# Delta-rule heads of a hybrid layer in two overlapped streams, decays masked by a minimum

## The chip, the cores and the metric

One core of a Trainium2 chip runs the whole program in one launch. The metric is the device time of one execution in microseconds; the median of three runs of the kernel before is 2117.78 us (2115.77 to 2118.18). Engines: TensorE (PE), VectorE (DVE), ScalarE (ACT), GpSimd (POOL) and SyncE (SP), which only issues DMAs. Each works through its own list of instructions in order and waits on semaphores.

## What is computed

512 positions of width 1024 go through a hybrid layer and two more layers with feed-forward blocks. All is fp32. Only the mixer of the first layer, `mix1`, bears on the change. It projects its normalized input, convolves over time, and runs two recurrences: a gated delta rule (8 heads) and a state-space model (SSD, 16 heads in 2 groups).

```python
def gdn_chunked(q, k, v, g, beta):   # heads of 128 x 128
    ...
    gc = jnp.cumsum(g, axis=-1)
    decay = jnp.exp(jnp.where(causal, gc[..., :, None] - gc[..., None, :], -jnp.inf))
    kb = k * beta[..., None]
    a_in = jnp.einsum("bhnid,bhnjd->bhnij", kb, k) * decay
    lmat = jnp.where(strict, a_in, 0.0) + jnp.eye(CHUNK, dtype=a_in.dtype)
    ...
    sol = lax.linalg.triangular_solve(lmat, rhs, left_side=True, lower=True, unit_diagonal=True)
    ...
    def step(state, xs):
        v_new = u_i - jnp.einsum("bhcd,bhde->bhce", w_i, state)
        o = jnp.einsum("bhcd,bhde->bhce", q_i, state) + jnp.einsum("bhij,bhje->bhie", qk_i, v_new)
        state = state * gl[..., None, None] + jnp.einsum("bhcd,bhce->bhde", k_i, v_new)
...
o_a = rms_norm(o_a, gdn_norm_w) * jax.nn.silu(z_a)
...
y = (ssd_chunked(xs_, dt, a_neg, bm, cm) + ssd_d * xs_) * jax.nn.silu(z_s)   # then rms_norm by group
mix = jnp.concatenate([o_a, o_s], axis=-1) @ w_out
x = x + rms_norm(mix, post_mix_norm)
```

## The kernel before

Activations lie as 8 blocks of 128 features by 512 positions, or, by "token", as 128 positions by 4 chunks. A projection multiplies fp32 data that are split into a high and a low part: three 512-column matmuls for each of 8 blocks (`mm3`, L214 to L216), 24 in all. Its weights come by `wload`: SP loads 512 KB (wr, L196), ACT casts the high part (wh, L202), DVE subtracts for the low part (wl, L205). `split1` does the same for activations (L295, L296).

`head_proj(h)` makes q, k and v of a head: projection, scaling on DVE (u, L466), a convolution with its first tap on ACT (L474) and three on DVE (L479), and SiLU on ACT (L691). `z_proj` makes the gate of a head, `zs_evac` those of SSD, `xbc` the inputs of SSD.

`gdn(h0, qkv)` is a generator for a pair of heads, cut by `yield` into stages. *Set-up:* k and q are transposed and squared (`sumsq`, L712), `kd` is k scaled by its decay (L729); `decay` makes exp(min(gc row - gc column, 0)) (L683, L684); B is k times k by decay and beta (L750); its 16x16 diagonal blocks are summed out (L754, L756), written to DRAM and read back rearranged (bdd: L757, L762, one write and eight reads on SP). Then PT is q times k by decay (L770), masked to the upper triangle on POOL (L771), and `nkv` is v scaled (L780). *Substitution:* 15 steps of two small DVE instructions solve the 16x16 blocks (L791, L792), and DVE spreads the result into Y (L801); PE transposes it to X (pX, L798). *Doubling:* X and Y grow to blocks of 32, 64 and 128 by products on PE (pT, pU, pY) with steps on DVE and ACT between them (L814 to L837). *Recurrence:* over four chunks, per head, PE forms k times state, DVE subtracts (r, L853), PE applies Y, DVE scales (vt, L856), PE forms the new state, DVE adds (L862 for chunk 0, L864); po is the output. *Output:* squares on ACT (L872), a root on DVE, product (L877), transposition (pfo, L880), gate (L882).

The loop over pairs drives a generator to the end of its substitution's inputs, and then, one stage at a time, writes projections between its stages as the table GF says: the next pair's heads, the z gates and the SSD gates all beside the substitution, doubling and recurrence of the same pair:

```python
GF = [[0], [1], [2, 3], []]
...
            for n in range(3):
                next(g)
            for n, fill in enumerate(GF):
                for x in fill:
                    ...
                if next(g, 1):
                    break
```

Then come the SSD inputs of group 0 (`ssd_proj`), `ssd_prep` (CB masked by a triangle on DVE, L947; x times dt on DVE, L957; xd = that by a decay on POOL, L960), `ssd_core` (states pS, L971; masked decays; y products py, L999, and po, L1002; norm; transposition pf, L1022), the inputs of group 1, and the output projection in three parts: `w_o1a` (delta-rule heads, splits alternating between DVE and POOL by PA), group 1's core, `w_o1b` (group 0, splits by PB_), `w_o1c` (group 1).

The order of the text is not the order of the engines: a list scheduler takes the instructions as they are written, with priorities by place (raised inside `high_priority`), and fixes one list for each engine. Tiles come from pools with a fixed number of buffers, so a buffer that is late to come free delays its next user.

Of the kernel before, what the change touches and what calls it, by code (L numbers as in the profile page):

```python
# [1 line left out]

# [38 lines left out]
for _n, _c in PV:  # L41
# [49 lines left out]
class Prog:  # L91
    def __init__(s, ctx, tc, a):
# [512 lines left out]
    def mix1(s, after):  # L605
# [290 lines left out]
        sc.activation(zs[0][:, :, 0:256], zs[0][:, :, 0:256], AF.Silu)  # L896

        nxt = [head_proj(0), head_proj(1)]
        for h0 in range(0, GDN_H, 2):
            g, nxt = gdn(h0, nxt), []  # L900
            for n in range(3):
                next(g)
            more = h0 + 2 < GDN_H
            for n, fill in enumerate(GF):
                for x in fill:
                    if x >= 2:
                        z_proj(h0 + x - 2)
                    elif more:
                        nxt.append(head_proj(h0 + 2 + x))
                    else:  # L910
                        for m in range(1 + x, 2 + 2 * x):
                            s.proj_tm([a["w_zs"][m - 1, 0], a["w_zs"][m - 1, 1]], acts, zs_evac(m))
                if next(g, 1):
                    break
            for _ in g:
                pass
# [651 lines left out]
```

## Time and profile before

| | before |
|---|---|
| median of 3 runs | 2117.78 us (2115.77 to 2118.18) |
| the profiled execution | 2123.84 us |
| its span, first to last instruction | 2122.1 us |
| busy: PE / DVE / ACT / POOL | 2078.7 / 1380.9 / 943.2 / 80.4 us |
| mean granted TensorE clock | 0.989 of 2.4 GHz |
| chain that ended last, by engine | PE 82%, DVE 8%, ACT 4%, DMA 3% |

The profiled execution is one more run, 0.3% above the median; its times are what the rows below give. A busy PE counts the time in which a matmul is under way, also at the lower clock; a granted clock of 1.00 is 2.4 GHz, 0.5 is 1.2 GHz, and values between them are means over a window. "Idle before <- releaser" says how long an engine stood still ahead of an instruction, and what it waited for.

### The profile page before, as it was taken

The numbers are of one execution on the slowest core, as the hardware profiler recorded it, in microseconds if no ns is written. First come the engines' busy times: TensorE is split into PE (matmuls) and PEld (weight loads), VectorE is DVE, ScalarE is ACT, GpSimd is POOL, SyncE is SP. The second block draws the span as 40 slices with busy tenths as digits, with TensorE's granted clock in tenths as the row PEclk, the third lists the DMA queues.
The fourth block names the chain that finished last, engine by engine and source line by source line (L and its number), as shares of the span: only waits on it lengthen the run. The fifth ranks groups of instructions, "written<-read, shape, count | busy, mean of one in ns | idle before, by whom it ended". The sixth has DMA issues, their size and how long they took to land.

```text
span 2122.1 us, 27151 instructions
## 1 busy us (share of the span) xinstructions
PE 2078.7 (98%) x10558; PEld 1734.2 (82%) x10558; DVE 1380.9 (65%) x2383; ACT 943.2 (44%) x1555; POOL 80.4 (4%) x79
## 2 busy tenths in 40 slices
PE   8989999999999999999999999999999999999999
PEld 7877898878888888888776888888879888888887
DVE  7858767787598776237997777753333676777621
ACT  7535435456455444235665444432252444444321
POOL 0000000111000000100001000001100010000000
PEclk9989999999999999999999999999999999999999
DMA  5323122133223223332111233233222122332332
GB/s 176 97 65 106 36 81 91 61 109 129 70 87 102 92 98 93 94 96 95 50 50 60 80 109 99 93 91 99 91 78 90 60 80 72 117 99 92 97 114 65
DMA packets 60358, 189.16 MB, mean 89 GB/s; under 512 B 7901, under 2 KB 13277, under 8 KB 60230
## 3 DMA queue, kind: packets, MB, share of 16 engines
q1 hardware_dynamic: 57874, 180.75, 26.6%
q0 software_dynamic: 2032, 6.59, 1.0%
q8 instruction: 83, 1.36, 0.3%
q14 instruction: 45, 0.37, 0.1%
q10 hardware_dynamic: 324, 0.09, 0.0%
HBM read 184.99 MB, written 2.41 MB: 88 GB/s over the span
## 4 chain that ended last, share of the span: by engine, by line
PE 82%; DVE 8%; ACT 4%; DMA 3%; issue 1%; POOL 0%; SPq 0%; ACTq 0%; DVEq 0%; POOLq 0%
PE pp L214 24%; PE pp L215 24%; PE pp L216 24%; DVE wl L205 2%; DMA wr<-in_w_qkvz 1%; DVE qkv L479 1%; PE pz L1124 1%; PE pU L819 1%; PE pT L812 1%; PE pS L1367 1%; ACT wh L202 1%; PE po L1376 1%; DMA a<-bdd 1%; ACT s L712 1%; PE py L999 0%
## 5 line engine op out<-in xcount | busy, mean ns | idle before, releaser
L214 PE MATMUL pp<-a,wh 128*128 128x512 f32 (+1 forms) x2128 | 823.1, 388 | 8.5 <-ACT a L326 2.4
L215 PE MATMUL pp<-a,wh 128*128 128x512 f32 (+1 forms) x2128 | 818.6, 385 | 4.2 <-DVE a L296 2.6
L216 PE MATMUL pp<-a,wl 128*128 128x512 f32 (+1 forms) x2128 | 817.5, 385 | 1.7 <-DVE wl L205 1.7
L202 ACT CAST wh<-wr 128x1024 fp32r<-128x1024 f32 (+3 forms) x327 | 336.6, 1031 | 513.7 <-PE pp L215 385.6
L205 DVE TENSOR_TENSOR wl<-wr,wh 128x1024 fp32r<-128x1024 f32 (+3 forms) x327 | 393.2, 1203 | 222.4 <-ACT wh L202 218.7
L214 PEld LDWEIGHTS pp<-a,wh 128*128 128x128 f32 x2128 | 402.7, 190 | 93.2 <-issue 6.8
L215 PEld LDWEIGHTS pp<-a,wh 128*128 128x128 f32 x2128 | 403.5, 190 | 84.0 <-DVE a L296 4.0
L216 PEld LDWEIGHTS pp<-a,wl 128*128 128x128 f32 x2128 | 403.0, 189 | 80.1 <-DVE wl L205 3.3
L466 DVE TENSOR_TENSOR u<-pp,rb 128x512 f32<-128x512 f32 x198 | 135.9, 688 | 165.8 <-PE pp L216 165.3
L479 DVE SCALAR_TENSOR_TENSOR c<-u,pv,c 128x511 f32<-128x511 f32 (+1 forms) x264 | 196.5, 748 | 3.9
L216 PE MATMUL pp<-t,wl 128*128 128x512 f32 (+1 forms) x336 | 130.9, 389 | 0.0
L214 PE MATMUL pp<-t,wh 128*128 128x512 f32 (+1 forms) x336 | 130.8, 389 | 0.0
L215 PE MATMUL pp<-t,wh 128*128 128x512 f32 (+1 forms) x336 | 129.7, 386 | 0.0
L214 PE MATMUL pp<-wh,a 128*128 128x256 f32 (+2 forms) x384 | 112.7, 295 | 7.4 <-ACT wh L355 4.8
L215 PE MATMUL pp<-wl,a 128*128 128x256 f32 (+2 forms) x384 | 112.2, 293 | 0.0
L216 PE MATMUL pp<-wh,a 128*128 128x256 f32 (+2 forms) x384 | 111.9, 292 | 0.0
L476 ACT ACTIVATE c<-u,pv 128x512 f32<-128x512 f32 x132 | 107.5, 815 | 9.0 <-DVE u L466 8.5
L499 ACT ACTIVATE c<-c 128x512 f32<-128x512 f32 x66 | 41.7, 632 | 106.5 <-DVE c L479 106.4
L214 PEld LDWEIGHTS pp<-wh,a 128*128 128x128 f32 x384 | 74.1, 194 | 9.7 <-ACT wh L355 4.8
L295 ACT CAST t<-c 128x512 fp32r<-128x512 f32 x42 | 26.1, 621 | 114.9 <-DVE c L500 114.9
L216 PEld LDWEIGHTS pp<-wh,a 128*128 128x128 f32 x384 | 74.3, 194 | 1.5 <-issue 1.4
L215 PEld LDWEIGHTS pp<-wl,a 128*128 128x128 f32 x384 | 74.2, 193 | 1.6 <-issue 1.2
(343 smaller groups left out, 2180.3 us busy)
## 6 DMA issues: line engine op xcount, KB each, us to landing
wr<-in_w_up SPq DMA_DIRECT2D x132, 512.0 KB
wr<-in_w_dn SPq DMA_DIRECT2D x48, 448.0 KB
wr<-in_w_qkvz SPq DMA_DIRECT2D x32, 512.0 KB
wr<-in_w_dn SPq DMA_DIRECT2D x24, 512.0 KB
t<-gcd POOLq DMA_DIRECT2D x24, 256.0 KB, 4.2
wr<-in_w_xbc SPq DMA_DIRECT2D x12, 512.0 KB
a<-bdd SPq DMA_DIRECT2D x32, 128.0 KB
wr<-in_w_o1a SPq DMA_DIRECT2D x8, 512.0 KB
```

The source lines that it names most:

```text
L202: nc.scalar.copy(hi[:, :f], raw[:, :f])
L205: e.tensor_tensor(lo[:, :f], raw[:, :f], hi[:, :f], ALU.subtract)
L214: mm(out, l[0], r[0], start=first, stop=False)
L215: mm(out, l[0], r[1], start=False, stop=False)
L216: mm(out, l[1], r[0], start=False, stop=last)
L295: nc.scalar.copy(hi, src)
L466: s.nc.vector.tensor_tensor(u, ps, rb, ALU.mult)
L476: nc.scalar.activation(c, u, AF.Identity, scale=w(taps - 1), bias=bias)
L479: nc.vector.scalar_tensor_tensor(c[:, sh:], u[:, :S - sh], w(j), c[:, sh:], ALU.mult, ALU.add)
L499: nc.scalar.activation(g, g, AF.Silu)
L712: sc.activation(j, pk[:, c, :], AF.Square, accum_out=out[:, col + c:col + c + 1])
L812: te.matmul(pT[:, c * 64:(c + 1) * 64], B[i][:, ch(c)], left(X[i][:, ch(c)], b), start=True, stop=True)
```

## The change

Line numbers of the changed kernel are 5 higher at L210, 14 to 20 higher in `gdn` and 31 higher at the end of SSD.

1. *Two streams.* The main loop drives two generators: g does the doubling, recurrence and output of pair p, n the set-up and substitution of pair p + 1, a stage of each in turn. GF is now a table by pair and stage of what is projected where: "h" a head, "z" a gate of a delta-rule head, "s" SSD gates, "x" SSD inputs. Group 0's SSD inputs are thereby projected beside the last pair.
2. *Decay.* L683 was subtract and minimum with 0; now it is one instruction with a tile `upto` (0 on and below the causal bound, -1e30 above) for the minimum, so the mask lies in the decay. The POOL mask of PT (L771) goes, and the DVE product that made CB becomes a copy on ACT.
3. *ACT for DVE.* `kd` and `nkv` are made by four scaled copies of 128 columns on ACT instead of one DVE product of 512, in tiles of another pool.
4. *POOL to DVE.* xd and four of the splits for the output projection.
5. *Priorities.* Cast and split of weights (HL), scaling of SSD inputs (HX), the splits and the first row of `w_o1a` (HA) are raised; the first head's split comes before group 0's core, the splits for `w_o1b` right after it.
6. *Tiles.* z0, the first SSD gates, lie in two tiles of the "act" pool; the triangle for the cumulative sums has its own load.

Instructions on DVE 2385 to 2379, on ACT 1432 to 1505, on POOL 84 to 64, on SP 403 to 404.

```diff
-    "mix1": [("tri", 128), ("lev", 2 * 64), ("b16", 8), ("i16", 16)],
+    "tri": [("tri", 128)],
+    "mix1": [("upto", 128), ("lev", 2 * 64), ("b16", 8), ("i16", 16)],
...
+    c["upto"] = np.where(i[:, None] <= i[None, :], 0.0, -1e30)
...
-        nc.scalar.copy(hi[:, :f], raw[:, :f])
...
-        e.tensor_tensor(lo[:, :f], raw[:, :f], hi[:, :f], ALU.subtract)
+        with s.tc.high_priority(offset=s.ahead):
+            nc.scalar.copy(hi[:, :f], raw[:, :f])
+            nc.vector.tensor_tensor(lo[:, :f], raw[:, :f], hi[:, :f], ALU.subtract)
...
-                v.tensor_scalar(r[:, c * P:(c + 1) * P], r[:, c * P:(c + 1) * P], gc3[:, c, h:h + 1], 0.0, ALU.subtract, ALU.min)
+                v.scalar_tensor_tensor(r[:, cs], r[:, cs], gc3[:, c, h:h + 1], s.c("upto"), ALU.subtract, ALU.min)
...
-                v.tensor_tensor(v3(kd[i]), ptk, dec3[:, :, h].unsqueeze(2).to_broadcast([P, NT, P]), ALU.mult)
+                for c in range(NT):
+                    sc.activation(kd[i][:, ch(c)], ptk[:, c, :], AF.Copy, scale=dec3[:, c, h:h + 1])
...
-                nc.gpsimd.tensor_tensor(v3(PT[i]), v3(PT[i]), tri_b, ALU.mult)
...
-                v.tensor_tensor(v3(nkv[i]), to_tok(vf[i]), nk[:, 4 * i:4 * i + 4].unsqueeze(2).to_broadcast([P, NT, P]), ALU.mult)
+                ptv = to_tok(vf[i])
+                for c in range(NT):
+                    sc.activation(nkv[i][:, ch(c)], ptv[:, c, :], AF.Copy, scale=nk[:, 4 * i + c:4 * i + c + 1])
...
+        heads, fs0 = {}, []
+        fill(0, 0)
+        g = gdn(0, [heads.pop(h)[0] for h in range(2)])
+        for n in range(4):
+            next(g)
+            fill(0, n + 1)
+        for p in range(4):
+            h1 = 2 * p + 2
+            n = gdn(h1, [heads.pop(h)[0] for h in (h1, h1 + 1)]) if p < 3 else iter([1] * 9)
+            for i in range(4):
+                next(g)
+                next(n)
+                fill(p + 1, i)
+            for _ in g:
+                pass
+            fill(p + 1, 4)
+            g = n
...
-            v.tensor_tensor(v3(CB), v3(pc), tri_b, ALU.mult)
+            sc.copy(CB, pc)
...
-                nc.gpsimd.tensor_tensor(v4(x3, 3), v4(x1)[:, 0:3], hb(dec3[:, 0:3, csl], 3), ALU.mult)
+                v.tensor_tensor(v4(x3, 3), v4(x1)[:, 0:3], hb(dec3[:, 0:3, csl], 3), ALU.mult)
...
+        pa = [s.split1(f) for f in oa[:NE]]
+        ssd_core(0, *ssd_prep(0, fs0, [s.act(F32) for _ in range(4)]))
+        hb4 = s.x8(F32R)
...
-GF = [[0], [1], [2, 3], []]
-PA = 0
-PB_ = 2
-WP = 0
+GF = ((("h0", "h1"), (), ("h2",), (), ("h3",)),
+      (("h4",), ("z0",), ("h5",), ("z1",), ()),
+      (("h6",), ("z2",), ("h7",), ("z3",), ()),
+      (("z4",), ("s1",), ("z5",), ("x8",), ("x10", "x0")),
+      (("z6",), ("s2",), ("z7",), ("s3",), ("x1", "x2", "x3")))
...
+NE = 1
+HA = 300
+HX = 300
+HL = 100
```

*First place: ACT in the first pair's substitution, before and now.* wh is a weight cast, qkv<-u,pv a convolution's first tap, qkv<-qkv its SiLU; x_617 is nkv of the first pair. The casts wh_1102 (before) and wh_1186 (now) are those of the first load that SP issues behind the bdd round trip.

```order
L474 ACTIVATE qkv_888<-u_886,pv 128x512
L691 ACTIVATE qkv_849<-qkv_849 128x512
L202 CAST wh_1102<-wr_1100 128x1024
L691 ACTIVATE qkv_888<-qkv_888 128x512
L474 ACTIVATE qkv_978<-u_976,pv 128x512
L691 ACTIVATE qkv_978<-qkv_978 128x512
L202 CAST wh_1136<-wr_1134 128x1024
```

Now, on ACT at the same place:

```order
L479 ACTIVATE qkv_853<-u_851,pv 128x512
L705 ACTIVATE qkv_814<-qkv_814 128x512
L705 ACTIVATE qkv_853<-qkv_853 128x512
L479 ACTIVATE qkv_992<-u_990,pv 128x512
L800 ACTIVATE x_617<-ps_890,s_886 128x128 x4
L800 ACTIVATE x_617<-ps_899,s_886 128x128 x4
L209 CAST wh_1186<-wr_1184 128x1024
L705 ACTIVATE qkv_992<-qkv_992 128x512
```

The tap of qkv_978 stood two rows behind the cast; that of qkv_992 (q of the fourth head in both) stands three rows ahead of it.

*Second place: DVE in the first pair's recurrence.* s<-rc are the recurrence's steps (r, vt, state), L801 and L821 the last substitution rows.

```order
L837 TENSOR_SCALAR t_929<-pU_1220 64x4x64
L837 TENSOR_SCALAR t_930<-pU_1226 64x4x64
L856 TENSOR_SCALAR s_1237<-rc_1235,s_672 128x128
L856 TENSOR_SCALAR s_1245<-rc_1243,s_672 128x128
L862 COPY s_1240<-rc_1235 128x128
L862 COPY s_1248<-rc_1243 128x128
L853 SCALAR_TENSOR_TENSOR s_1253<-rc_1251,s_426,t_763 128x128
L853 SCALAR_TENSOR_TENSOR s_1265<-rc_1263,s_426,t_770 128x128
L856 TENSOR_SCALAR s_1256<-rc_1251,s_672 128x128
L856 TENSOR_SCALAR s_1268<-rc_1263,s_672 128x128
```

Now, on DVE, where chunk 1 begins:

```order
L821 TENSOR_TENSOR t_1674<-s_1639,cmix_283 128x512
L821 TENSOR_TENSOR t_1675<-s_1639,cmix_283 128x512
L806 COPY s_3083<-cmix_283 128x128
L873 SCALAR_TENSOR_TENSOR s_1726<-rc_1724,s_432,x_617 128x128
L873 SCALAR_TENSOR_TENSOR s_1738<-rc_1736,s_432,x_617 128x128
L876 TENSOR_SCALAR s_1729<-rc_1724,s_684 128x128
L876 TENSOR_SCALAR s_1741<-rc_1736,s_684 128x128
L471 TENSOR_TENSOR u_1977<-pp_1952,rb_366 128x512
L884 SCALAR_TENSOR_TENSOR s_1732<-s_1628,s_430,rc_1724 128x128
L884 SCALAR_TENSOR_TENSOR s_1744<-s_1636,s_430,rc_1736 128x128
L210 TENSOR_TENSOR wl_2268<-wr_2265,wh_2267 128x1024
L873 SCALAR_TENSOR_TENSOR s_1750<-rc_1748,s_432,x_617 128x128
```

Before, r of chunk 1 (L853) followed chunk 0 directly, with the next pair not yet set up. Now it (L873) stands behind the last substitution rows of the next pair (t_1674, t_1675); foreign rows among the ten are u_1977 and wl_2268.

*Third place: PE at the end of SSD group 1.* pf is the transposition of group 1's output, pp_4803 and pp_4856 products of `w_o1a`, pp_5162 (before), pp_5199 and pp_5247 (now) products of `w_o1b`.

```order
L214 MATMUL pp_4803<-a_4562,wh_4799 128x512
L1022 MATMUL pf_5111<-cst,a_4527 128x128 x2
L215 MATMUL pp_4803<-a_4563,wh_4799 128x512
L216 MATMUL pp_4803<-a_4562,wl_4800 128x512
L1022 MATMUL pf_5111<-cst,a_4527 128x128 x2
L1022 MATMUL pf_5122<-cst,a_4528 128x128 x4
L1022 MATMUL pf_5133<-cst,a_4529 128x128 x4
L214 MATMUL pp_5162<-a_5140,wh_5158 128x512
```

Now, on PE, behind the last po of group 1:

```order
L1033 MATMUL po_5116<-t_4953,xbc_4421 128x128
L221 MATMUL pp_4856<-a_4615,wl_4853 128x512
L1033 MATMUL po_5116<-t_4961,xbc_4421 128x128
L219 MATMUL pp_5199<-x_4336,wh_5195 128x512
L220 MATMUL pp_5199<-t_4337,wh_5195 128x512
```

And on PE where the first pf stands:

```order
L219 MATMUL pp_5247<-x_4336,wh_5229 128x512
L220 MATMUL pp_5247<-t_4340,wh_5229 128x512
L221 MATMUL pp_5247<-x_4336,wl_5230 128x512
L1053 MATMUL pf_5153<-cst,a_4583 128x128
L219 MATMUL pp_5247<-x_4336,wh_5229 128x512
L1053 MATMUL pf_5153<-cst,a_4583 128x128
```

Before, `w_o1b` began behind the last pf. Now 42 of its matmuls stand ahead of the first pf, and the others lie among the pf (the two pieces are the start and the end of those 42).

## Rows read from the trace of the kernel before

**Rows 1.** The page, part 1: busy us, share of the span, instructions.

```profile
PE 2078.7 (98%) x10558; PEld 1734.2 (82%) x10558; DVE 1380.9 (65%) x2383; ACT 943.2 (44%) x1555; POOL 80.4 (4%) x79
```

**Rows 2.** Window: length, busy PE PEld DVE ACT POOL, PEclk, DMA share, GB/s.

```profile
40.00:540.00 500.00, 476.91 (x2804) 407.61 (x2803) 372.77 (x861) 246.06 (x574) 39.67 (x48) 0.97 0.28 87
```

**Rows 3.** Windows by stage of the first layer, the same columns.

```profile
113.00:138.00 25.00, 24.21 (x146) 21.59 (x146) 7.04 (x15) 5.93 (x10) 0.54 (x1) 0.73 0.17 50
138.00:160.00 22.00, 21.87 (x133) 19.14 (x132) 17.47 (x47) 7.85 (x23) 0.00 (x0) 1.00 0.17 53
...
183.00:207.00 24.00, 21.46 (x95) 17.46 (x93) 20.96 (x51) 10.21 (x15) 0.00 (x0) 1.00 0.54 165
207.00:228.00 21.00, 20.46 (x148) 17.59 (x149) 8.77 (x16) 5.91 (x10) 0.54 (x1) 0.92 0.14 34
...
347.00:374.00 27.00, 24.61 (x102) 19.29 (x100) 21.76 (x51) 10.25 (x13) 0.00 (x0) 0.94 0.47 156
415.00:457.00 42.00, 40.93 (x250) 35.48 (x249) 37.77 (x82) 24.33 (x57) 10.86 (x17) 1.00 0.25 80
457.00:473.00 16.00, 11.34 (x35) 7.22 (x34) 16.00 (x30) 9.33 (x24) 5.45 (x3) 0.85 0.40 133
473.00:500.00 27.00, 25.97 (x145) 21.22 (x144) 16.24 (x33) 20.46 (x41) 6.88 (x9) 0.97 0.38 127
528.00:540.00 12.00, 9.66 (x33) 6.14 (x32) 4.00 (x6) 11.90 (x29) 0.00 (x0) 0.72 0.19 57
```

**Rows 4.** Timeline of PE, first and second X: start, us, instruction, [idle <- releaser].

```profile
107.83 0.39 PE L215 MATMUL pp<-a,wh 128*128 128x512 f32 x1
108.06 0.39 PE L216 MATMUL pp<-a,wl 128*128 128x512 f32 x1
113.79 1.11 PE L798 MATMUL pX<-cst,t 128*128 128x128 f32 x4 [5.35 <-DVE t L801]
...
207.54 0.65 PE L798 MATMUL pX<-cst,t 128*128 128x128 f32 x4 [3.08 <-DVE t L801]
```

**Rows 5.** Timeline of DVE in the first substitution.

```profile
94.64 0.75 DVE L479 SCALAR_TENSOR_TENSOR qkv<-u,pv,qkv 128x511 f32<-128x511 f32 x1 [4.03 <-ACT qkv L474]
95.31 0.25 DVE L791 TENSOR_TENSOR s<-a,s 128x96 f32<-128x96 f32 x1
```

**Rows 6.** Timeline of ACT in the first substitution.

```profile
92.42 1.05 ACT L202 CAST wh<-wr 128x1024 fp32r<-128x1024 f32 x1 [5.71 <-DMA wr<-in_w_qkvz]
```

**Rows 7.** Timeline of SP in the first substitution.

```profile
80.61 5.08 SPq L762 DMA_DIRECT2D a<-bdd  x8
85.81 5.03 SPq L196 DMA_DIRECT2D wr<-in_w_qkvz  x2
```

**Rows 8.** Waits of SP, 40 to 540 us: total us, times, longest.

```profile
SPq L757 <- DVE s L756: 65.5, 4, 24.2
```

**Rows 9.** By line: count, ns min/median/max, first and last start, forms.

```profile
L683 DVE TENSOR_SCALAR t<-t,s x96: 273/282/590, 67.7 to 511.9; 128x128 f32<-128x128 f32 x96
...
L853 DVE SCALAR_TENSOR_TENSOR s<-rc,s,t x24: 344/351/354, 140.6 to 402.9; 128x128 f32<-128x128 f32 x24
...
L479 DVE SCALAR_TENSOR_TENSOR xbc<-u,pv,xbc x36: 730/746/1756, 357.0 to 470.8; 128x511 f32<-128x511 f32 x12, 128x510 f32<-128x510 f32 x12, 128x509 f32<-128x509 f32 x12
...
L791 DVE TENSOR_TENSOR s<-a,s x60: 168/226/285, 85.0 to 371.7; 128x120 f32<-128x120 f32 x4, 128x112 f32<-128x112 f32 x4, 128x104 f32<-128x104 f32 x4, 128x96 f32<-128x96 f32 x4
...
L205 DVE TENSOR_TENSOR wl<-wr,wh x327: 725/1224/2317, 18.2 to 2099.0; 128x1024 fp32r<-128x1024 f32 x136, 128x896 fp32r<-128x896 f32 x24, 128x768 fp32r<-128x768 f32 x2, 128x816 fp32r<-128x816 f32 x1
...
L780 DVE TENSOR_TENSOR t<-ps,s x8: 673/681/690, 78.8 to 345.9; 128x512 f32<-128x512 f32 x8
...
L296 POOL TENSOR_TENSOR a<-a,a x4: 1519/1786/2337, 450.3 to 468.6; 128x512 fp32r<-128x512 f32 x4
...
L960 POOL TENSOR_TENSOR xd<-t,s x8: 832/1020/1813, 417.9 to 486.1; 128x384 f32<-128x384 f32 x8
...
L712 ACT ACTIVATE s<-ps x64: 255/320/387, 60.8 to 327.8; 128x128 f32<-128x128 f32 x64
```

More of the change, by code (lines that the diff above doesn't have):

```diff
@@ L1 @@
 from contextlib import ExitStack
+from itertools import chain
 import numpy as np
@@ L102, in __init__ @@
         s.pre, s.ready = [], []
-        s.nw, s.wpool = 0, 0
+        s.ahead = 0
         nc = s.nc
@@ L609, in mix1 @@
         acts, R, rb = s.start()
-        s.wpool = WP
+        s.ahead = HL
         rv = s.cp.tile([P, 64], F32, name="rv")
@@ L614, in mix1 @@
         ident = s.c("ident")
-        tri_b = s.c("tri").unsqueeze(1).to_broadcast([P, NT, P])
         def v3(t, n=NT):
             return t.rearrange("p (a b) -> p a b", a=n)
-        zs = [s.x8(), s.x8()]
+        z0 = [s.act(F32) for _ in range(2)]
+        zs = [None, None]
         def zs_evac(m):
+            if zs[m // 2] is None:
+                zs[m // 2] = s.x8()
             def f(tb, ps):
@@ L631, in mix1 @@
             v.tensor_scalar(sp3[:, tb, :], ps[:, 256:288], R[:, tb:tb + 1], None, ALU.mult)
-            sc.activation(zs[0][:, tb, 0:256], ps[:, 0:256], AF.Copy, scale=R[:, tb:tb + 1])
+            for j in range(2):
+                sc.activation(z0[j][:, tb * P:(tb + 1) * P], ps[:, j * P:(j + 1) * P], AF.Copy, scale=R[:, tb:tb + 1])
         beta = s.small(32, tag="beta", bufs=1)
@@ L720, in gdn @@
             hs, I = (h0, h0 + 1), range(2)
+            if h0 + 2 < GDN_H:
+                K4 = s.x8()
+                K4 = [K4[:, i, :] for i in range(4)]
+            else:
+                K4 = [s.act(F32) for _ in range(4)]
+            kd, nkv = K4[:2], K4[2:]
             qf, kf, vf = zip(*qkv)
@@ L894, in head_proj @@
             return [qkv_proj(h), qkv_proj(8 + h), qkv_proj(16 + h)]
[L896 to L916, printed above, removed]
+        for z in z0:
+            sc.activation(z, z, AF.Silu)
         def xbc(m):
             ps = s.proj_fm([(a["w_xbc"][m], KB)], acts)
-            u = s.scaled(ps, rb)
+            with s.tc.high_priority(offset=HX):
+                u = s.scaled(ps, rb)
             c = s.conv(u, lambda j: s.p("ssd_cw", m * 4 + j), 4, bias=s.p("ssd_cb", m), out=s.t(tag="q", role="xbc"))
@@ L924, in xbc, with zs_proj, fill @@
             return c
+        def zs_proj(m):
+            s.proj_tm([a["w_zs"][m - 1, 0], a["w_zs"][m - 1, 1]], acts, zs_evac(m))
+        def fill(p, n):
+            for x in GF[p][n]:
+                if x[0] == "h":
+                    heads.setdefault(x[1], []).append(head_proj(x[1]))
+                else:
+                    {"z": z_proj, "s": zs_proj, "x": lambda m: fs0.append(xbc(m))}[x[0]](x[1])
+        heads, fs0 = {}, []
[15 more added lines that the diff above has]
+            g = n
         os_ = []
@@ L1025, in ssd_core @@
                 os_.append(of)
-        ssd_core(0, *ssd_prep(0, ssd_proj(0), [s.act(F32) for _ in range(4)]))
+        pa = [s.split1(f) for f in oa[:NE]]
+        ssd_core(0, *ssd_prep(0, fs0, [s.act(F32) for _ in range(4)]))
+        hb4 = s.x8(F32R)
+        pb = []
+        for i, f in enumerate(os_):
+            pb.append((hb4[:, i, :], s.t(F32R)))
+            sc.copy(pb[i][0], f)
+            v.tensor_tensor(pb[i][1], f, pb[i][0], ALU.subtract)
         fs = ssd_proj(1)
@@ L1033, in mix1 @@
         p0 = s.tc.cur_priority
-        pa = [s.split1(f, pool=i % 2 == PA) for i, f in enumerate(oa)]
+        with s.tc.high_priority(offset=HA):
+            pa += [s.split1(f) for f in oa[NE:]]
+            part_a = s.proj_part(a["w_o1a"], 1, 8, pa)
+            first = next(part_a)
         F = []
-        for m, ps in s.proj_part(a["w_o1a"], 1, 8, pa):
+        for m, ps in chain([first], part_a):
             f = s.act(F32)
@@ L1049, in mix1 @@
             nc.sync.dma_start(X[k], a["x_t"][k])
-        s.wpool = 0
+        s.ahead = 0
         s.log_exp()
```

20 lines of the change are left out of this document (10 added, 10 removed).

## The prediction

> **What bounds the kernel now.** The page comes first: the matrix engine (PE) is busy 98% of the span and VectorE (DVE) 65%, so only time in which PE stands still or runs slowly can be won [rows 1]. The change touches the first layer alone (from the start to about 600 us of 2122), and its PE work is the same, 9828 matmuls in both programs. So I read that layer by windows: from 40 to 540 us PE is busy 476.9 of 500 us at a mean granted clock of 0.97 [rows 2]. That is 23.1 us idle and (1 - 0.97) x 500 = 15 us of clock: **some 38 us are all there is to win.** The stage rows [rows 3] show where: holes, and behind them stretches at the lower clock (1.2 GHz). In order of time:
>
> - *First substitution.* PE issues a 512-column matmul every 0.23 us, stops after 108.06 and goes on at 113.79: 5.5 us, in which it waits for DVE's last substitution row (t, L801) [rows 4]. DVE was late because it stood still for 4.03 us, up to 94.64, waiting for a convolution's first tap on ScalarE (ACT) [rows 5]. That tap (L474) was queued behind a weight cast (L202, 92.42), which had waited 5.71 us for its load [rows 6]; and SyncE (SP) issued that load only at 85.81, in order behind the reads of the bdd round trip [rows 7]. Then the clock: 0.73 over the next 25 us means that (1 - 0.73)/0.5 = 54% of them, 13.5 us, ran at 1.2 GHz. That costs 6.75 us if PE alone sets the pace, less where the doubling's chain through DVE and ACT sets it; I take 5.
> - *Second substitution.* The same wait, 3.1 us [rows 4], then 0.08 x 21 = 1.7 us of clock: 4.8. *Fourth:* 2.4 idle and 0.06 x 27 = 1.6 of clock: 4.0. The third's is smaller.
> - *SSD group 0.* 1.1 idle from 415 to 457, 4.7 from there to 473, and 0.15 x 16 = 2.4 of clock: 8.2 us. DVE is 100% busy in the last 16 us.
> - *SSD group 1.* 1.0 idle at 473 to 500; at 528 to 540 2.3 idle and 0.28 x 12 = 3.4 of clock, 5.7 us.
>
> **The change, part by part**, by the new order of instructions and these durations.
>
> *First substitution.* On ACT the tap of the conv now stands ahead of the cast that waits for the load behind bdd (first place in the section on the change), so the 4.0 us stall goes. DVE's work from the second head's L750 to the last substitution row grows by 3.0 us of durations: one more conv step (0.75) and weight split (1.22), one more product each at L770 and L772 (0.68 each), six small ones (1.0), less two products at L780 (1.36) that go to ACT [rows 9]. About 2 of the 3 count, since neighbours overlap by some 0.1 us. PE has 0.7 us more to do. So 5.5 - 4.0 + 2.0 - 0.7 leaves a hole of 2.8 us, and I set 1.5 for the clock behind it. Saved: 10.5 - 4.3 = **6.2**.
>
> *The other substitutions* run beside the former pair's doubling and recurrence. Between the second pair's first products and its X, PE now has 28.9 us of work (106 projection matmuls at 0.227 and 28 short ones), DVE 24.9: the hole and its clock go, **4.8**. Third: PE 31 us, DVE 20; I take nothing. Fourth: 27.7 us on PE; I leave 1 of 4.0, **3.0**. On SP, bdd is what can hold back other loads: it waited up to 24.2 us for L756 [rows 8], with all that is queued behind it. In the new order the loads behind it are wanted some 32 us later, and need about 13.5; I take nothing.
>
> *The recurrence.* Its later chunks now stand on DVE behind the next pair's substitution (second place), so its last po comes later, and between that po and pfo PE needs other work. There stand 31 full projection matmuls for the first pair (7.0 us), 38 half-width ones for the second (4.5), 4.9 and 8.2 us for the others. The chain is eight squares (0.32), ten small steps of the root (0.17) and two products (0.68) [rows 9]: 5.7 us, and up to 8.8 where ACT or DVE is shared. Holes of about 0, 1.1, 0.8 and 0.6: **-2.5**. PE had other work there before.
>
> *SSD 0.* From the first x product to the last split for the output projection DVE has 55.2 us to do: 32 decays (0.29), 10 conv steps (0.75), 4 weight splits (1.22), 37 products of 512 columns (0.68), 12 of 384 (0.55) and small ones. PE has 53.4 there: 173 projection matmuls and 14.1 us of short ones. DVE remains just the bound. But splits that alternated between DVE and POOL (four there, 1.79 us each) and four xd (1.02) leave POOL, and the CB product leaves DVE [rows 9]. I leave 3.7 of 8.2, **4.5**.
>
> *SSD 1.* xd on DVE ends the wait for POOL's xd, **0.9**. At its end 42 matmuls of the second output projection (9.5 us) stand ahead of the first pf (third place), where PE before had only pf to wait for. I leave 1.7 of 5.7, **4.0**.
>
> *Decay.* 96 instructions of 0.282 us (L683) get a second SBUF operand. Below, they cost nothing more; above, 0.351 us, the same kind of instruction from PSUM (L853). Nearest is L479, that kind with two fp32 SBUF operands: 0.746 us for 511 columns; with L791, also of two, 0.285 for 120, that is 1.18 ns a column and 0.29 us for 128 [rows 9]. I take 0.29: 0.3 us more over SSD 0's 32, counted above; by the upper bound 2.2. The Trainium skill (Vector Engine (DVE) Microarchitecture Reference, "Points that are easy to get wrong") has this form run at half throughput when both SBUF sources are not bf16. A second pass over 128 columns at 1.18 ns would add 0.15 us to each, 4.8 us to DVE in SSD 0, and the sum would be 16.1 instead of 20.9. L479's rate in this trace speaks against it.
>
> *The rest.* ACT gets 64 scaled copies for 16 products of DVE: at 0.32 us (L712) 20.5 us over the layer, to 246 of 500 us busy [rows 2, 9]: hidden. If ACT were full in a set-up, each pair would come up to 5.1 us later. The mask that leaves POOL held up nobody, and z0's split copies and one more constant load lie in the start-up: nothing.
>
> **Sum:** 6.2 + 4.8 + 3.0 - 2.5 + 4.5 + 0.9 + 4.0 = 20.9 us. The profiled execution took 2123.84 us (its span is 1.7 less), so the changed one would take 2102.9. The median of the runs lies 6.1 below it: **2097 us**.
>
> **The rivals.**
>
> *Slower: the recurrence falls behind foreign work on DVE.* Its chain has ten hops per pair from PE over DVE and back. If each waits behind one weight split of the other stream (1.22 us), 40 hops cost 49 us against 20.9 gained: 2146 us. It decides from 17 hops on. For it: one queue serves both streams, and the splits are raised in priority. Against: in the new order only some three of the first pair's hops have a foreign row between them; and before, such rows stood there too, with PE busy 21.87 of 22 us from 138 to 160 [rows 3].
>
> *Only the ends gain.* The holes of the substitutions move to doubling and recurrence, which lose their fills; what stays is the SSD part and 2 us of the first hole: 4.5 + 0.9 + 4.0 + 2 = 11 us, 2106. For it: the -2.5 above, and a DVE that is 75% busy in the layer [rows 2].
>
> *Nearly all goes.* The clock never falls from 79 to 540 us and only short waits are left: 36 us, 2082.
>
> *No change:* holes of the same sum in other places, 2118. That the streams don't overlap at all is excluded by the order.
>
> **How the numbers follow.** My forecast with gains of 15 to 29 us (2089 to 2103) has 0.50; only the ends (2103 to 2113) 0.18; nearly all (2077 to 2089) 0.17; no change 0.06; the slower rival 0.09. A measurement of this kernel can tell 0.2%, 4.2 us, from no change. So faster 0.85, same 0.06, slower 0.09. The range takes in the first three cases: 2077 to 2112. The bounds of the clock after the first hole (4 to 6.75) and of the decay lie within it.
>
> **What would show it.** Right: no PE wait over 3 us for the first or second X; the clock at 1.00 from the second substitution to the fourth and at the end of SSD 1; pf of group 1 beside projection matmuls; L683's successor near 0.29 us. Wrong: PE or its weight loads waiting for L853, L856 or L864 by more than a microsecond; a hole ahead of pfo in each pair; casts that wait for loads behind bdd; DVE full through the doubling. If a decay takes 0.43 us, the page's rule holds, and SSD 0 keeps its hole.

## The result and the profile after

The changed kernel takes **2093.74 us** (median of 4 runs, 2091.98 to 2097.55) against 2117.98 of the kernel before (2115.77 to 2118.24): ratio 0.9885, 95% interval 0.9872 to 0.9898, 24.2 us less. The forecast was 2097, the range 2077 to 2112. The profiled execution of the changed kernel took 2093.87 us, near its median; that of the kernel before lay 6 us above its own, so the two spans (2092.1 and 2122.1) differ by more than the medians.

Page of the changed kernel, part 1, beside [rows 1]:

```profile
PE 2060.9 (99%) x10558; PEld 1723.3 (82%) x10558; DVE 1374.1 (66%) x2377; ACT 964.5 (46%) x1628; POOL 53.7 (3%) x59
```

PE is busy 17.8 us less for the same matmuls. That is clock: a matmul at 1.2 GHz is busy for longer (the four of an X below take 0.63 us at a clock of 1.00, and 1.09 us at the third X, in a low stretch), and the mean granted clock went from 0.989 to 0.997, so (1 - 0.989) x 2122 - (1 - 0.997) x 2092 = 17 us. The window that answers to [rows 2], and 20 us windows of the changed kernel (start:end, length, busy us of PE, PEld, DVE, ACT, POOL, PEclk, DMA share, GB/s):

```profile
40.00:540.00 500.00, 489.00 (x2943) 421.86 (x2942) 384.29 (x883) 275.43 (x652) 13.32 (x28) 0.99 0.29 91
...
100.00:120.00 20.00, 18.90 (x112) 15.96 (x111) 15.12 (x37) 9.07 (x13) 0.00 (x0) 1.00 0.36 105
120.00:140.00 20.00, 20.00 (x148) 17.13 (x147) 12.46 (x40) 14.34 (x52) 0.00 (x0) 1.00 0.08 28
180.00:200.00 20.00, 19.92 (x126) 17.15 (x124) 14.48 (x34) 11.90 (x46) 0.00 (x0) 1.00 0.24 75
240.00:260.00 20.00, 15.37 (x103) 14.66 (x102) 14.78 (x45) 4.84 (x8) 0.88 (x2) 0.83 0.23 79
320.00:340.00 20.00, 18.04 (x133) 17.10 (x131) 12.18 (x43) 6.74 (x24) 0.00 (x0) 0.91 0.14 48
420.00:440.00 20.00, 18.86 (x106) 16.05 (x105) 18.07 (x40) 11.10 (x40) 1.36 (x5) 1.00 0.09 27
460.00:480.00 20.00, 20.00 (x117) 16.94 (x116) 16.59 (x29) 15.48 (x31) 2.68 (x5) 1.00 0.52 166
520.00:540.00 20.00, 20.00 (x106) 16.90 (x106) 12.52 (x18) 12.39 (x21) 0.00 (x0) 1.00 0.41 135
```

Of the 500 us, 11.0 are idle (23.1 before), and of its 25 windows of 20 us two alone have a clock below 1.00: (1 - 0.83) x 20 + (1 - 0.91) x 20 = 5.2 us lost, where before it was some 17 by the same windows (15 by the two digits of [rows 2]). Together that is 24 of the 30 us between the two spans. Some of the rest is not the change's: from 1540 to 1600 us, in a later layer that it leaves alone, the kernel before lost 5 us of clock in its profiled execution, the changed one less than 2. Both windows with a lower clock are those of an X. Timeline of PE in the changed kernel at the four X (columns as in [rows 4], whose rows at 113.79 and 207.54 are the first and the second X before):

```profile
109.98 0.63 PE L818 MATMUL pX<-cst,t 128*128 128x128 f32 x4 [1.10 <-DVE t L821]
...
168.08 0.63 PE L818 MATMUL pX<-cst,t 128*128 128x128 f32 x4 [0.34 <-DVE t L821]
...
247.99 1.09 PE L818 MATMUL pX<-cst,t 128*128 128x128 f32 x4 [4.63 <-DVE t L821]
...
322.93 0.66 PE L818 MATMUL pX<-cst,t 128*128 128x128 f32 x4 [1.89 <-DVE t L821]
```

The first X waits 1.1 us (5.35 before), the second 0.3 (3.08). But the third waits 4.6 (0.3 before) and the fourth 1.9. Before, the fourth X, at 373.58, did not wait at all: of the 2.4 us idle from 347 to 374 that the prediction counted as its hole, 1.9 were a wait for a weight cast some 13 us earlier (timeline of PE, kernel before), and the rest one for a low part just behind it.

```profile
360.12 0.50 PE L214 MATMUL pp<-a,wh 128*128 128x512 f32 x1 [1.86 <-ACT wh L202]
```

Why the third X now waits, the timelines of SP, ACT and DVE of the changed kernel show, in this order:

```profile
225.70 4.95 SPq L782 DMA_DIRECT2D a<-bdd  x8
230.75 0.40 SPq L202 DMA_DIRECT2D wr<-in_w_zs  x1
```
```profile
237.90 1.05 ACT L209 CAST wh<-wr 128x1024 fp32r<-128x1024 f32 x1 [5.74 <-DMA wr<-in_w_zs]
```
```profile
234.73 0.25 DVE L811 TENSOR_TENSOR s<-a,s 128x88 f32<-128x88 f32 x1
238.98 1.23 DVE L210 TENSOR_TENSOR wl<-wr,wh 128x1024 fp32r<-128x1024 f32 x1 [4.00 <-ACT wh L209]
240.12 0.25 DVE L812 TENSOR_TENSOR s<-s,s 128x88 f32<-128x88 f32 x1
```

It is the chain of [rows 5 to 7] once more, one place on: SP issues an SSD gate's weights (w_zs) only behind the eight bdd reads, the cast waits 5.74 us for them, and the split (L210) behind that cast stands in DVE's list between two steps of the substitution (L811, L812), so DVE stands still for 4.00 us and X comes later by as much.

### The profile page after: what moved, and what is told of

Same layout as the page of the kernel before. It is cut to its first block, busy times and chain, and to the rows that moved or that the text cites. A ratio compares the mean times of both kernels' runs of the same rounds, so it can differ in the third digit from the quotient of the medians.

```text
span 2092.1 us, 27148 instructions
## 1 busy us (share of the span) xinstructions
PE 2060.9 (99%) x10558; PEld 1723.3 (82%) x10558; DVE 1374.1 (66%) x2377; ACT 964.5 (46%) x1628; POOL 53.7 (3%) x59
## 4 chain that ended last, share of the span: by engine, by line
PE 86%; DVE 8%; ACT 3%; DMA 2%; issue 1%; SPq 0%; ACTq 0%; DVEq 0%
PE pp L219 25%; PE pp L221 25%; PE pp L220 25%; DVE qkv L484 1%; DVE wl L210 1%; DMA wr<-in_w_qkvz 1%; PE pz L1164 1%; PE pS L1407 1%; PE pT L832 1%; PE py L1030 1%; PE pU L839 1%; PE po L1416 1%; PE po L1213 1%; ACT wh L209 0%; DVE u L471 0%
## 5 line engine op out<-in xcount | busy, mean ns | idle before, releaser
L219 PE MATMUL pp<-a,wh 128*128 128x512 f32 (+1 forms) x2096 | 805.9, 386 | 4.9 <-ACT a L331 2.4
L221 PE MATMUL pp<-a,wl 128*128 128x512 f32 (+1 forms) x2096 | 800.4, 382 | 1.9 <-DVE wl L210 1.9
L220 PE MATMUL pp<-a,wh 128*128 128x512 f32 (+1 forms) x2096 | 800.4, 382 | 0.0
L210 DVE TENSOR_TENSOR wl<-wr,wh 128x1024 fp32r<-128x1024 f32 (+3 forms) x327 | 392.4, 1201 | 231.1 <-ACT wh L209 227.1
L219 PEld LDWEIGHTS pp<-a,wh 128*128 128x128 f32 x2096 | 393.7, 188 | 83.7 <-issue 4.0
L221 PEld LDWEIGHTS pp<-a,wl 128*128 128x128 f32 x2096 | 394.4, 188 | 77.7 <-DVE wl L210 2.7
L220 PEld LDWEIGHTS pp<-a,wh 128*128 128x128 f32 x2096 | 394.6, 188 | 76.7 <-issue 4.4
L471 DVE TENSOR_TENSOR u<-pp,rb 128x512 f32<-128x512 f32 x198 | 135.8, 687 | 162.8 <-PE pp L221 162.4
L484 DVE SCALAR_TENSOR_TENSOR c<-u,pv,c 128x511 f32<-128x511 f32 (+1 forms) x264 | 196.3, 747 | 3.9
L220 PE MATMUL pp<-t,wh 128*128 128x512 f32 (+1 forms) x368 | 142.7, 388 | 0.0
L219 PE MATMUL pp<-t,wh 128*128 128x512 f32 (+1 forms) x336 | 130.8, 389 | 0.0
L219 PEld LDWEIGHTS pp<-wh,a 128*128 128x128 f32 x384 | 74.7, 195 | 8.7 <-ACT wh L360 4.9
L220 PEld LDWEIGHTS pp<-t,wh 128*128 128x128 f32 x368 | 69.1, 188 | 15.2
```

Source lines behind the costliest of these rows:

```text
L210: nc.vector.tensor_tensor(lo[:, :f], raw[:, :f], hi[:, :f], ALU.subtract)
L219: mm(out, l[0], r[0], start=first, stop=False)
L220: mm(out, l[0], r[1], start=False, stop=False)
L221: mm(out, l[1], r[0], start=False, stop=last)
L471: s.nc.vector.tensor_tensor(u, ps, rb, ALU.mult)
L484: nc.vector.scalar_tensor_tensor(c[:, sh:], u[:, :S - sh], w(j), c[:, sh:], ALU.mult, ALU.add)
```

## The experiments

All are built on the changed kernel unless it is said otherwise. They ran in three lots of four (e1 to e4, e5 to e8, e9 to e12), each beside the kernel before, at 2119.2, 2119.1 and 2121.2 us; the ratios are to these, so kernels of different lots are compared by their ratios, and with the changed kernel's 0.9885.

### The main parts, one at a time

**e1_serial.** In the loop over pairs, and GF as a table for it:

```diff
-            n = gdn(h1, [heads.pop(h)[0] for h in (h1, h1 + 1)]) if p < 3 else iter([1] * 9)
-            for i in range(4):
-                next(g)
-                next(n)
-                fill(p + 1, i)
+            g = gdn(2 * p, [heads.pop(h)[0] for h in (2 * p, 2 * p + 1)])
+            for _ in range(3):
+                next(g)
+            for i in range(4):
+                fill(p + 1, i)
+                if next(g, 1):
+                    break
...
+        for m in (8, 10, 0, 1, 2, 3):
+            fs0.append(xbc(m))
```

> The changed kernel with one part undone: the pairs run one after the other again, with the fills beside the same pair as in the kernel before; every other edit stays. Theory (the sum of the prediction): overlap carries 4.8 + 3.0 - 2.5 of the gain, so some 5 us are lost, 2097 to 2103 us, with waits of PE of about 3 us at the second X and at a fourth one. Rival A (the side edits do it all): 2094 within 3 us. Rival B (overlap is most of the gain): 2108 us or more.

2118.48 us (ratio 1.0012, 0.9988 to 1.0035): all of the gain is gone, rival B. The waits of PE (us in total, times, longest):

```profile
PE pX L818 <- DVE t L821: 15.7, 4, 4.6
...
PE pp L221 <- DVE wl L210: 3.7, 2, 3.0
```

Each of the four X waits, 15.7 us in all (8.8 in the kernel before, 8.0 in the changed one), and PE waits 3.0 us for one weight split in SSD 0 (from 460 to 480 us), where the conv steps of SSD's inputs are back and DVE is busy 17.75 of 20 us. The edit undoes two things: the streams, and the place of group 0's SSD inputs, which go behind the last pair again. No run tells these apart; the waits at the X belong to the first.

**e2_before_ssd.** The kernel before, with the SSD part of the change:

```diff
-                nc.gpsimd.tensor_tensor(v4(x3, 3), ...)
+                v.tensor_tensor(v4(x3, 3), ...)
...
-        pa = [s.split1(f, pool=i % 2 == PA) for i, f in enumerate(oa)]
+        with s.tc.high_priority(offset=300):
+            pa = [s.split1(f) for f in oa]
```

and the splits pb made from `os_` ahead of `ssd_proj(1)`.

> The kernel before with the SSD part alone: xd and all splits for the output projection on DVE, the splits of the first projection part raised, those of group 0's outputs made right after its core. Theory: 4.5 + 0.9 + 4.0 us gained, 2107 to 2111 us, clock 1.00 at 528 to 540 us. Rival (only the ends gain, the whole gain lies here): 2100 us or less. Rival (these holes come from DVE's load and move): 2115 us or more.

2116.70 us (0.9992, 0.9977 to 1.0008): no gain that can be told, the second rival. Its profiled execution, the fastest of its ten, took 2109.41 us, so its windows show the better case. The end of SSD 1 is mended there, as its windows show beside [rows 3]; SSD 0 is not:

```profile
440.00:460.00 20.00, 16.29 (x87) 13.89 (x86) 18.77 (x44) 14.43 (x41) 0.00 (x0) 0.91 0.00 0
460.00:480.00 20.00, 18.12 (x101) 14.20 (x100) 15.44 (x28) 16.67 (x37) 1.06 (x2) 1.00 0.24 80
520.00:540.00 20.00, 19.87 (x95) 15.85 (x94) 11.73 (x27) 15.22 (x37) 0.00 (x0) 1.00 0.31 90
```

DVE is nearly full at 440 to 460 us (as it was at 457 to 473 before), and PE stands for 3.7 of the 20 us, with a lower clock. So taking POOL out of SSD 0 is not enough. What is left on DVE there, and is not in the changed kernel, are the conv steps of group 0's inputs, which now lie beside the fourth pair; that this frees SSD 0 is argued from the lists and from e1_serial, not tried alone.

**e3_no_raise.**

```diff
-HL = 100
+HL = 0
```

> The changed kernel with HL = 0: casts and splits of weights keep the priority of their place. Theory (the wait of 4.6 us at the third X comes from a load queued behind the bdd reads, and the raise only sets where its split stands among the substitution steps): a move of the hole by some us either way, 2090 to 2097 us. Rival A (the raise puts the split in front of the steps and makes the hole): 2085 to 2089 us. Rival B (the raise is what feeds PE): 2098 us or more.

2119.34 us (1.0004, 0.9993 to 1.0015): rival B, far beyond its figure; without the raise the two streams, with all else of the change, are worth nothing. Its waits of PE, and from its timeline of DVE the rows for the longest:

```profile
PE pp L221 <- DVE wl L210: 14.2, 5, 9.9
PE pX L818 <- DVE t L821: 10.8, 3, 4.1
```
```profile
449.83 0.74 DVE L484 SCALAR_TENSOR_TENSOR xbc<-u,pv,xbc 128x511 f32<-128x511 f32 x1
...
458.62 2.35 DVE L210 TENSOR_TENSOR wl<-wr,wh 128x1024 fp32r<-128x1024 f32 x2
```

PE stops for 9.9 us, for one low part (wl) whose split stands on DVE behind twelve conv steps, from 449.83 on, and comes at 458.62. At the X, too, DVE waits for late casts (3.5, 3.1 and 2.7 us ahead of three of them) and the X for DVE.

**e10_o1b_late.** The six lines that make `hb4` and `pb` stand behind `ssd_core(1, ...)`.

> The changed kernel with the splits of group 0's outputs written behind group 1's core, as before; all else stays. By the prediction's sum 4.0 us are lost at the end of SSD 1 (pf without projection matmuls beside it): 2096 to 2100 us, a hole and a lower clock before 530 us. Rival (the scheduler finds other work there now): 2092 to 2095 us.

2113.07 us (0.9961, 0.9946 to 0.9976): 16 us lost by the ratios, not 4. At the end of SSD 1, its timeline of PE and its windows:

```profile
517.96 1.89 PE L1053 MATMUL pf<-cst,a 128*128 128x128 f32 x6 [5.19 <-issue]
```
```profile
500.00:520.00 20.00, 14.41 (x82) 11.64 (x80) 16.16 (x39) 10.48 (x38) 0.00 (x0) 0.90 0.35 122
520.00:540.00 20.00, 18.70 (x67) 14.35 (x68) 7.79 (x10) 10.36 (x20) 0.00 (x0) 0.76 0.09 29
```

5.2 us without work ahead of pf, then (1 - 0.90) x 20 + (1 - 0.76) x 20 = 6.8 us of clock, and 1.3 more idle: 13 us lie in these two windows (the changed kernel loses nothing in its window there). So the prediction's cause holds, and its price was three times too small. The profiled execution also lost some 4 us by the fourth X (327.16 us there, 322.93 in the changed kernel), though the instruction lists of PE, DVE, ACT and SP are the same up to that place; that is not the edit's.

**e11_no_hx_ha.**

```diff
-HA = 300
-HX = 300
+HA = 0
+HX = 0
```

> The changed kernel with HA = HX = 0: the scaling of SSD inputs and the splits and first row of the first output projection keep the priority of their place; the raise of the weights' casts and splits stays. Theory (as with the weights: what PE waits for stands behind convolutions on DVE): 3 to 9 us lost around 380 to 460 us, 2097 to 2103. Rival (the raise of the weights is enough): 2092 to 2096 us.

2107.20 us (0.9939, 0.9921 to 0.9956): 11 us lost by the ratios, more than expected, and where expected. PE waits 5.32 us for the scaling (u, L471) of an SSD input, which stood behind SSD's own products and conv steps on DVE (timeline of PE, then windows):

```profile
437.87 0.77 PE L219 MATMUL pp<-a,wh 128*128 128x512 f32 x1 [5.32 <-DVE u L471]
```
```profile
420.00:440.00 20.00, 14.68 (x83) 12.61 (x82) 17.54 (x36) 10.50 (x35) 0.10 (x1) 0.89 0.08 26
440.00:460.00 20.00, 19.43 (x98) 15.68 (x97) 15.86 (x35) 15.64 (x33) 0.54 (x2) 0.94 0.27 81
```

**e7_pool_back.**

```diff
-                v.tensor_tensor(v4(x3, 3), ...)
+                nc.gpsimd.tensor_tensor(v4(x3, 3), ...)
...
-        pa = [s.split1(f) for f in oa[:NE]]
+        pa = [s.split1(f, pool=True) for f in oa[:NE]]
...
-            pa += [s.split1(f) for f in oa[NE:]]
+            pa += [s.split1(f, pool=i % 2 == 1) for i, f in enumerate(oa[NE:])]
```

> The changed kernel with POOL's share of the SSD part as before: xd and every second split for the output projection on POOL. By the sum of the prediction 4.5 + 0.9 us are lost: 2097 to 2101 us, with PE waiting for POOL in the SSD part. Rival (the SSD part gains by what runs beside the last pair, not by POOL; the run that moved this work alone gained nothing): 2092 to 2096 us.

2102.82 us (0.9913, 0.9895 to 0.9932): some 6 us lost by the ratios, near the 5.4 of the sum, with intervals that just touch (the changed kernel's ends at 0.9898). In e2_before_ssd the same edit and two more gained nothing that can be told. The splits on POOL took 1.47 us and xd 1.05 (by line: ns min/median/max, first and last start):

```profile
L301 POOL TENSOR_TENSOR a<-a,a x4: 1302/1472/1676, 395.2 to 455.3; 128x512 fp32r<-128x512 f32 x4
...
L991 POOL TENSOR_TENSOR xd<-t,s x8: 832/1054/1817, 403.7 to 478.7; 128x384 f32<-128x384 f32 x8
```

The profiled execution is 10.5 us longer than that of the changed kernel, but 4.4 of these are lost by its fourth X (timeline of PE; 322.93 in the changed kernel), where the instruction lists are still the same. Behind it PE waits 0.6 us for a split on POOL (its waits of PE, 360 to 600 us).

```profile
327.34 0.69 PE L818 MATMUL pX<-cst,t 128*128 128x128 f32 x4 [2.04 <-DVE t L821]
```
```profile
PE pp L220 <- POOL a L301: 0.6, 1, 0.6
```

**e5_dve_scales and e6_old_decay.**

```diff
-                    sc.activation(kd[i][:, ch(c)], ptk[:, c, :], AF.Copy, scale=dec3[:, c, h:h + 1])
+                v.tensor_tensor(v3(kd[i]), ptk, dec3[:, :, h]..., ALU.mult)
```

(nkv alike); and for e6, with the triangle kept as a constant:

```diff
-                v.scalar_tensor_tensor(r[:, cs], r[:, cs], gc3[:, c, h:h + 1], s.c("upto"), ALU.subtract, ALU.min)
+                v.tensor_scalar(r[:, cs], r[:, cs], gc3[:, c, h:h + 1], 0.0, ALU.subtract, ALU.min)
...
+                nc.gpsimd.tensor_tensor(v3(PT[i]), v3(PT[i]), tri_b, ALU.mult)
...
-            sc.copy(CB, pc)
+            v.tensor_tensor(v3(CB), v3(pc), tri_b, ALU.mult)
```

> The changed kernel with kd and nkv made by one DVE product of 512 columns again (16 x 0.68 us) instead of four scaled copies on ACT (64 x 0.40 us in the trace of the changed kernel). Theory: DVE's 11 us more lie partly ahead of the substitutions and make their holes larger: 2095 to 2100 us. Rival A (DVE sets the pace of the whole layer): 2103 us or more. Rival B (hidden, since PE has other work there): 2092 to 2095 us.

> The changed kernel with the decays of the kernel before: minimum with 0 (0.282 us each instead of 0.345 in the trace of the changed one), the mask of PT on POOL (8 x 1.29 us) and CB masked by a DVE product (2 x 0.69). Theory: DVE wins 6.0 us of 384 and loses 1.4, nobody waits for the mask on POOL: no difference beyond 3 us, 2091 to 2097. Rival A (the decays hold up the SSD part, as they would at half throughput): 2090 us or less. Rival B (PT now waits for POOL, or POOL slows DVE): 2098 us or more.

2094.80 us (0.9883, 0.9868 to 0.9898) and 2092.93 us (0.9875, 0.9860 to 0.9890): neither can be told from the changed kernel. For e5 that is rival B: work moved between ACT and DVE is hidden both ways. For e6 it is the theory: in this kernel the form of the decay is worth nothing.

### The wait at the third X

Four kernels tried to take it away.

```diff
e4_bdd_pool_queue
-            nc.sync.dma_start(bdd.rearrange(...
+            nc.gpsimd.dma_start(bdd.rearrange(...
...
-                    nc.sync.dma_start(t_[:, 256 * i:256 * i + 256],
+                    nc.gpsimd.dma_start(t_[:, 256 * i:256 * i + 256],
e8_bdd_merged_pool (with e4)
-            bdd = s.dr.tile([2, P, 64], F32, ...
+            bdd = s.dr.tile([32, 2, 4, 64], F32, ...
...
-                for i in I:
...
+                nc.gpsimd.dma_start(t_, bdd.rearrange("(m z) i j c -> m z (i j c)", z=4)[:, z]...
e9_three_loads (e12_pool_queue_three_loads: with e4)
-NBUF = {"act": 32, "wr": 2, "wh": 4, "wl": 4}
+NBUF = {"act": 32, "wr": 3, "wh": 4, "wl": 3}
```

> The changed kernel with the bdd round trip (one write and eight reads a pair) issued from POOL's queue instead of SP's, so no weight load is queued behind it. Theory: the casts at the third X no longer wait for a late load, DVE's 4.0 us stall and PE's 4.6 us go with their lower clock, the same at the fourth: 2084 to 2089 us. Rival (POOL issues nine transfers more slowly, the substitutions begin later): 2094 us or more, with DVE waiting for a<-bdd ahead of the first step.

> The changed kernel with the bdd round trip on POOL's queue and rearranged in DRAM, so that two writes and four reads do instead of one and eight. Theory (with the round trip away from SP the fourth X waits 3.0 us for the eight reads, so fewer reads take that hole away): 2086 to 2090 us. Rival (the hole moves to the next late thing, DVE's convolutions): 2091 to 2094 us.

> The changed kernel with three buffers for raw weights instead of two, and three for their low parts instead of four (the memory allows no more). Theory: loads go out one further ahead, so fewer of them lie behind the bdd round trip when their cast is due; the holes at the first, third and fourth X shrink: 2086 to 2091 us. Rival A (the third low-part buffer is what is short): splits come later, 2097 us or more. Rival B (neither): 2092 to 2096 us.

> The two changes on loads together: bdd on POOL's queue and three raw-weight buffers (three low-part buffers). Theory: no load waits behind bdd and each has one more stage of lead; the holes at X shrink to a microsecond, 2084 to 2089 us. Rival (the holes move to the reads of bdd on POOL and to DVE's own work, as with the merged reads): 2090 to 2095 us.

2092.32 us (0.9881, 0.9855 to 0.9907), 2094.19 (0.9878, 0.9863 to 0.9893), 2094.94 (0.9883, 0.9862 to 0.9903) and 2096.98 (0.9887, 0.9868 to 0.9906): none is told from the changed kernel's 0.9885, and the further gain of 5 us and more did not come. In e4 the third X waits 1.6 us instead of 4.6, as the theory said, but the fourth waits 3.6 instead of 1.9: there DVE waits for the reads themselves (its timeline of DVE; its waits of PE).

```profile
304.32 0.28 DVE L811 TENSOR_TENSOR s<-a,s 128x120 f32<-128x120 f32 x1 [3.01 <-DMA a<-bdd]
```
```profile
PE pX L818 <- DVE t L821: 7.0, 4, 3.6
```

The four X wait 7.0 us in all where they wait 8.0 in the changed kernel, and 7.8 in e8: there the holes move, and their sum hardly falls. With three raw-weight buffers it does, to 4.1 (e9) and 4.3 us (e12), and up to 540 us e12 has the gain that its theory asked for (its waits of PE, 36 to 600 us; its windows):

```profile
PE pX L818 <- DVE t L821: 4.3, 3, 2.0
```
```profile
40.00:540.00 500.00, 492.77 (x2996) 425.18 (x2995) 386.97 (x888) 276.98 (x657) 35.67 (x64) 1.00 0.31 91
540.00:640.00 100.00, 95.14 (x525) 83.52 (x524) 86.17 (x156) 53.42 (x82) 0.00 (x0) 0.97 0.28 86
1060.00:1080.00 20.00, 17.41 (x67) 12.78 (x66) 17.04 (x37) 9.50 (x18) 0.00 (x0) 0.83 0.07 21
```

Up to 540 us 7.2 us are idle at full clock, where the changed kernel loses 11.0 and 5.2 of clock. But NBUF sets the buffers of the whole program: behind 540 us both e9 and e12 fall to 0.97 and 0.83 in windows in which the changed kernel stays at 1.00, and what was won is lost again. Three buffers in the first layer alone were not tried.

## Why the prediction was right

The sum was 20.9 us, measured were 24.2. By its terms:

- *First substitution (6.2):* larger, 5.5 + 5 less 1.1 us in this execution, and the clock stays 1.00 behind it. The reason holds (the tap ahead of the cast): DVE's stall for the tap is gone. But how large it came out is in part luck: in e7 and e10, with the same lists up to there, the first X waited 3.5 us with 1.7 of clock, because loads landed later, and that is near the 4.3 that the sum left.
- *Second (4.8):* right, 0.34 us left and no lower clock.
- *Third (0) and fourth (3.0):* **wrong.** The step that failed is "In the new order the loads behind it are wanted some 32 us later, and need about 13.5; I take nothing": a load behind bdd was late (issued 230.75, cast 237.90), and it was its raised split, not PE's want of the weights, that stopped DVE. The third X cost 4.6 us and 3.4 of clock, the fourth 1.9 and 1.8: some 12 us, where the sum left 1 and the third's small hole. The fourth's 4.0 were misread besides: that hole was a wait for a cast at 360 us and not one of the X. It went; the wait at the fourth X is new.
- *Recurrence (-2.5):* too dark. The one wait of PE for pfo in the changed kernel is short (waits of PE, 36 to 600 us):

```profile
PE pfo L900 <- DVE t L897: 0.4, 1, 0.4
```

- *SSD 0 (4.5) and SSD 1 (0.9 + 4.0):* too small. At 420 to 440 us 1.1 us are left, at 460 to 480 and 520 to 540 nothing, all at full clock: some 13 us instead of 9.4. And the reason given for SSD 0 does not suffice: e2 has the same moves from POOL and keeps the hole. The early splits are worth more in this kernel than the hole that they closed (5.7 us before): without them e10 loses 13 us there.
- *Decay:* 0.29 us was taken, between 0.282 and 0.351; it took 0.345 (changed kernel, by line):

```profile
L697 DVE SCALAR_TENSOR_TENSOR t<-t,s,cmix x96: 339/345/352, 53.5 to 500.8; 128x128 f32<-128x128 f32 x96
```

  That is 6 us more on DVE in the layer, but e6 shows it to be worth nothing there. The 1.18 ns a column came from a line through two kinds of instruction, L479 and L791. By one kind, L697 and L484 (0.75 us for 511 columns), a column costs (0.75 - 0.345)/383 = 1.06 ns. The rule of the Trainium skill (Vector Engine (DVE) Microarchitecture Reference, "Points that are easy to get wrong"), which the prediction read as a second pass of 0.15 us, would by that reading have asked for 0.43 here: the measurement decides against the reading. The rule itself isn't refuted. Two instructions of L683's kind, with one SBUF operand and a constant, show a column at less (kernel before, by line):

```profile
L636 DVE TENSOR_SCALAR s<-s x1: 172/172/172, 30.4 to 30.4; 128x32 f32<-128x32 f32 x1
```
```profile
L664 DVE TENSOR_SCALAR s<-s x1: 210/210/210, 43.0 to 43.0; 128x96 f32<-128x96 f32 x1
```

  That is (0.210 - 0.172)/64 = 0.59 ns. If L683 ran at that rate, the new form has little more than half of it, and 128 x (1.06 - 0.59) ns = 0.06 us is all that it costs more. No run has L683 at another width, so this stays an estimate.
- *ACT's copies* took 0.44 and 0.38 us instead of 0.32, hidden, as e5 shows.

So the total came out by errors that cancel: about 9 us missed at the third and fourth X, and about as much more won at the first X, ahead of pfo and in SSD. That is luck in the number; the mechanism was right for the first and second X and the end of SSD 1, and incomplete for SSD 0. Of its own signs of being wrong one came true, casts that wait for loads behind bdd, and of its signs of being right two failed: the clock fell at the third and fourth X, and a decay took 0.345 us.

And one thing the sum had no room for: it treated the parts as independent. Undone one at a time, the parts cost, by the ratios, 27 us (streams), 25 (raised splits), 16 (splits of group 0 early), 11 (other raises) and 6 (POOL), some 86 us in all for a change worth 24. About 4 of the 16 and of the 6 may be late loads at the X, as the profiled executions of e10 and e7 have them. Without the streams or without the raise nothing of the gain stands; without one of the others a third to three quarters of it do. Why, the windows above show: PE goes through one list, so one late operand anywhere opens a hole (3 to 10 us in the rows above), and most of these are followed by several microseconds at 1.2 GHz; where two streams share a list, what is late in one can stop the other. The slower rival named that danger (DVE's list serving both), but on the wrong side: it saw raised splits ahead of the recurrence as the risk, while e3 shows splits that are *not* raised, behind convolutions, to be the dearer case. The raised split that stopped DVE for 4.0 us at the third X is the danger that it named, in the substitution instead of the recurrence.

"Only the ends gain" is refuted by e1 and e2, "nearly all goes" by the third and fourth X; e12 comes near it up to 540 us and loses it behind.

## What to carry to other kernels

Where two streams share in-order engines, first look at what the bottleneck engine waits for (weights' low parts, scaled inputs) and give just that a priority over both streams: overlap alone was worth nothing here without it. Undo each part of such a change alone before you believe a sum of terms, and look in the trace whether the loss lies where the edit is: some 4 us of what e7 and e10 lost came ahead of it. And a load that stands in a queue behind a transfer which waits for a computation is a hole waiting to happen; moving the transfer off the queue helps only if what it feeds isn't late next.

## What was not expected

- The kernel before spreads from 2112.2 to 2123.0 us over 25 runs, with mean granted clocks of 0.990 to 0.996, and e1_serial from 2114.9 to 2135.0 over ten. What sets this was not tried. The changed kernel has four runs only, from 2092.0 to 2097.6; they don't show whether it is steadier.
- Up to the SSD part e7 has the same instruction lists on PE, DVE, ACT and SP as the changed kernel, and yet its first X waited 3.5 us, not 1.1. From 76 to 112 us its casts waited for loads for 6.0 us, those of the changed kernel for 1.0 (waits of ACT, the changed kernel first); e10 shows the same 6.0:

```profile
ACT wh L209 <- DMA wr<-in_w_qkvz: 1.0, 2, 0.5
```
```profile
ACT wh L209 <- DMA wr<-in_w_qkvz: 6.0, 3, 3.6
```

  So a hole of some microseconds at an X can come and go between executions with the landing of a load; what sets that was not tried.
